# Three of the 44 weight units of the gated product in other matmul forms: 512 columns, 384 columns, and two row tiles per block

## The chip, the cores and the metric

The kernel runs on one core of one Trainium2 chip. The metric is the device time of one execution in microseconds (us). The engines are TensorE (PE in the rows, with its weight loads as PEld), VectorE (DVE), ScalarE (ACT), GpSimd (POOL) and SyncE (SP), which issues most DMAs.

## The reference, cut to what matters

One layer of a hybrid decoder runs over 520 columns of activations (512 prompt tokens and 8 sample tokens) of width 1024. Three branches are merged and normed into h. Then comes a gated feed-forward part, and the change lies in its first product:

```python
u, new_ffn = causal_dwconv(h @ prm['w_ffn_in'], ffn_buf, prm['ffn_dw'], prm['ffn_dw_b'])   # 1024 -> 2*2816
f = (jax.nn.silu(u[..., :D_FF]) * u[..., D_FF:]) @ prm['w_ffn_out']                        # 2816 -> 1024
out = layer_norm(ALPHA * h + f, prm['ln2_g'], prm['ln2_b'])
```

## The kernel before

**Units.** Activations lie transposed, features on the 128 partitions and the 520 columns free. `w_ffn_in` is cut into 44 weight units (i = 0 to 43) of 128 output features; even ones belong to the gate, odd ones to the other factor. A unit holds eight 128x128 blocks. Weights and activations are each split into a rounded part and a remainder (`hi`, `lo`, type fp32r), and each block is multiplied three times: hi by hi, hi by lo, lo by hi. The 520 columns are worked as two halves of HB = 260. So a unit is two halves of 24 matmuls with 260 columns, first all of half 0, then all of half 1 (`mm3`), each half adding up in a PSUM bank of its own.

**Banks.** All these products take their banks from the pool `pd`, three in all (`PD = 3`), handed out in turn (`dps`). A bank given out anew waits until the readers of its tile before have ended, so the n-th tile waits for the (n-3)-th. Each unit takes two, so unit 8's halves take the banks of unit 6's half 1 and unit 7's half 0, and so on.

**Around a unit.** `wunit` loads the unit by a DMA on SP (`raw`), ScalarE rounds it to `whi`, VectorE makes `wlo`; two buffers each, so the weights of unit i+2 are split when unit i's last matmul is done. `ffn_evac` empties the banks with four instructions of ScalarE: two copies into `u` (tile `fu`) and two scaled and biased ones into `y` (`fy`), halves 0 and 1 each. `ffn_taps` is the convolution along the columns on VectorE. Then come silu, the product of both factors, and the split into `f`, the input of the second product. Units 0 to 5 are handled ahead, half 0 of all, then half 1 of all (`early`).

**Order.** Within TensorE the dense matmuls are chained in the order of the program (`issue_after(last_mm)`). The order of the instructions on ScalarE and VectorE is laid out when the kernel is built, by a planner that simulates the engines and goes by priorities; `hp()` raises one (weight splits, evacuations), dense matmuls have the lowest (`-LOW`). An engine then works in that fixed order.

Of the kernel before, what the change touches and what calls it, by code (L numbers as in the profile page):

```python
# [9 lines left out]
F32 = mybir.dt.float32  # L10
F32R = mybir.dt.float32r
AF = mybir.ActivationFunctionType
ALU = mybir.AluOpType
# [3 lines left out]
HB = 260  # L17
# [99 lines left out]
def build(tc, nc, I, O):  # L117
    V, S, T, G = nc.vector, nc.scalar, nc.tensor, nc.gpsimd
# [4 lines left out]
    LOW = 100000  # L123
# [6 lines left out]
    def hp(more=0):  # L130
        return tc.high_priority(HP + more)
# [6 lines left out]
    pd = st.enter_context(tc.tile_pool(name="pd", bufs=PD, space=bass.MemoryType.PSUM))  # L138
# [6 lines left out]
    def z2(name, shape=(128, NT), dt=F32):  # L145
        return pool.tile(list(shape), dt, tag="z", bufs=NZ, name=name)
# [13 lines left out]
    def act(out, in_, func=AF.Copy, **kw):  # L160
        return S.activation(out, in_, func, **kw)  # L161

    def tt(out, a, b, op):
        return V.tensor_tensor(out, a, b, op=op)  # L164
# [19 lines left out]
    HS = (slice(0, HB), slice(HB, NT))  # L184
# [53 lines left out]
    def wload(src, n):  # L238
        raw = wp.tile([128, 8, 128], F32, tag="raw", bufs=2, name="raw")
        with tc.issue_after(x_load.ins):  # L240
            ins = nc.sync.dma_start(raw[:, :n].rearrange("p k m -> p (k m)"), src)
        nload[0] += 1
        if nload[0] > 1 and late:
            with tc.issue_after(ins.ins):
                late.popleft()()
        elif nload[0] > 6:
            with tc.issue_after(ins.ins):
                cache_step(2 if nload[0] % 3 == 0 else 1)
        return raw

    def wsplit(raw, n, where=None):

        if where is None:
            where = [[wp.tile([128, 8, 128], F32R, tag=t, name=t) for t in ("whi", "wlo")]]
        ks, k0 = [], 0
        for hi, lo in where:
            m = min(hi.shape[1], n - k0)
            if m > 0:
                split(hi[:, :m], lo[:, :m], raw[:, k0:k0 + m])
                ks += [(hi[:, k], lo[:, k]) for k in range(m)]  # L260
            k0 += m
        return ks

    def wunit(src, n, where=None):
        with hp():
            return wsplit(wload(src, n), n, where)
# [8 lines left out]
    with hp():  # L275
# [3 lines left out]
        for k in range(8):  # L279
            xr = t2(f"xr{k}")  # L280
            x_load = nc.sync.dma_start(xr, I['xT'][:, k, :])
            if k < 2:
                q = slice(4 * k, 4 * k + 4)
# [5 lines left out]
    def P(name, i=0, n=1):  # L289
        o = PPO[name] + i  # L290
        return pp[:, o:o + n]
# [52 lines left out]
    last_mm, last_one, nmm, stages = [None], [None], [0], deque()  # L344

    def mm3(ps, w, X, first, last, halves):
        for i, h in enumerate(halves):
            for k, ((hi, lo), (xh, xl)) in enumerate(zip(w, X)):
                for q, (a, x) in enumerate(((hi, xh), (hi, xl), (lo, xh))):
                    with ExitStack() as es:  # L350
                        if last_mm[0] is not None:
                            es.enter_context(tc.issue_after(last_mm[0].ins))
                        nmm[0] += 1
                        if stages and nmm[0] >= NS:
                            es.enter_context(tc.issue_after(stages.popleft().ins))
                            nmm[0] = 0
                        last_mm[0] = T.matmul(ps[i], lhsT=a, rhs=x[:, HS[h]], start=first and k == 0 and q == 0,  # L357
                                              stop=last and k == len(w) - 1 and q == 2)

    def dps(n=2):  # L360
        return [pd.tile([128, 512], F32, tag="d", name="ps")[:, :HB] for h in range(n)]


    def densemm(ps, w, X, first=True, last=True, halves=(0, 1)):
        with tc.high_priority(-LOW):
            mm3(ps, w, X, first, last, halves)

    def dense(w, X):
        ps = dps()
        densemm(ps, w, X)  # L370
        return ps

    zi = [0]

    def zchunk():
        i = zi[0]
        zi[0] += 1
        w = w0 if i == 0 else wunit(I['wz'][i], 8)
        return dense(w, XS)
# [737 lines left out]
    def stream_dense():  # L1117
# [61 lines left out]
        def branch(i, js, na):  # L1179
            br = B_ORDER[i]  # L1180
            wn, X, n, ev = outs[br]
            ahead = []
            for j in js[:na]:
                ahead.append(gate(br, j))
                yield 6.5
            yield ('w', ev)
            for j in js:
                gt = ahead[j] if j < len(ahead) else gate(br, j)
                w = wunit(I[wn][j], n)
                pb = dense(w, X)  # L1190
                if i == 0:
                    mg.append(gt)
                if i == 2:
                    XM.append((t2(f"m{j}h", dt=F32R), t2(f"m{j}l", dt=F32R)))
                with hp():
                    for h in range(2):
                        stt(gt[:, HS[h]], gt[:, HS[h]], 1.0, pb[h], ALU.add, ALU.mult)

                for sl in HS if i == 2 and j == 7 else (slice(0, NT),):
                    if i:  # L1200
                        tt(mg[j][:, sl], mg[j][:, sl], gt[:, sl], ALU.add)
                    if i == 2:
                        hi, lo = [x[:, sl] for x in XM[j]]
                        act(hi, mg[j][:, sl], scale=0.5)
                        last_m[0] = stt(lo, mg[j][:, sl], 0.5, hi.bitcast(F32), ALU.mult, ALU.subtract)
                yield 6.5 + 0.8 * n
# [184 lines left out]
    XH = [(h_hi[:, j, :], h_lo[:, j, :]) for j in range(8)]  # L1391
# [29 lines left out]
    def ffn_taps(c, u, y):  # L1421
        G.tensor_copy(nu[:, c, :], u[:, 510:520])  # L1422
        tt(y[:, 512:520], y[:, 512:520], sfs[:, c, :], ALU.add)
        stt(y[:, 1:512], u[:, 0:511], P('fdw', c * 3 + 1), y[:, 1:512])
        stt(y[:, 2:512], u[:, 0:510], P('fdw', c * 3 + 0), y[:, 2:512])

    def ffn_evac(c, u, y, ps, halves):
        with hp():
            for h, p_ in zip(halves, ps):
                act(u[:, HS[h]], p_)  # L1430
            for h, p_ in zip(halves, ps):
                act(y[:, HS[h]], p_, AF.Identity, scale=P('fdw', c * 3 + 2), bias=P('fdb', c))
# [4 lines left out]
    for h in range(2):  # L1437
        for i in range(NH):
            w, u, y = early[i]
            ps = dps(1)  # L1440
# [6 lines left out]
    def ffn_chunk(c, i):  # L1447
        if i < NH:
            _, u, y = early[i]
        else:  # L1450
            u, y = z2("fu"), z2("fy")
            ffn_evac(c, u, y, dense(wunit(I['wfi'][i], 8), XH), (0, 1))
        ffn_taps(c, u, y)
        return y

    for i in range(22):
        yg = ffn_chunk(i, 2 * i)
        act(yg, yg, AF.Silu)
        yu = ffn_chunk(22 + i, 2 * i + 1)
        tt(yg, yg, yu, ALU.mult)  # L1460
        hi, lo = [t(f"f{i}", dt=F32R) for t in FT[i]]
        split(hi, lo, yg)
        XF.append((hi, lo))
# [123 lines left out]
```

## Time and profile before

| | us |
|---|---|
| median of 3 runs | 1034.26 (1032.29 to 1035.23) |
| profiled execution, its own time | 1034.04 |
| its span in the trace | 1032.3 |
| TensorE busy | 1007.8 (98%) |
| VectorE busy | 710.0 (69%) |
| ScalarE busy | 515.5 (50%) |
| mean granted TensorE clock | 0.993 |

Matmul records overlap each other: one record is some 280 ns long, while the next begins about 120 ns after it. So a busy share near one says that the engine is never empty, and the distance between starts says how fast it goes.

### The profile page before, as it was taken

How to read it: one execution, taken by the hardware profiler on the slowest of the kernel's cores; microseconds unless marked ns; L12 is line 12 of the kernel's file. 1: busy time of each engine (PE TensorE's matmuls, PEld its weight loads, DVE VectorE, ACT ScalarE, POOL GpSimd, SP SyncE). 2: the span in 40 equal slices, each digit the busy share in tenths (PEclk: the TensorE clock that was granted, in tenths of full speed). 3: DMA queues.
4: the chain of work that ended last, by engine and by line, in shares of the span. 5: the costliest groups of instructions: out<-in, count | busy, mean ns of one | idle time of the engine just before them, and what ended most of it. 6: DMA issues, size and time to landing. Idle time of an engine off the chain costs nothing.

```text
span 1032.3 us, 22347 instructions
## 1 busy us (share of the span) xinstructions
PE 1007.8 (98%) x9091; PEld 981.7 (95%) x9091; DVE 710.0 (69%) x1330; ACT 515.5 (50%) x1071; POOL 222.1 (22%) x314
## 2 busy tenths in 40 slices
PE   7999999999999998999999999999999999999995
PEld 7999999999999898889989999999999999999994
DVE  5999899986586699745557688655666556423376
ACT  6255843574543534434544567555555555322264
POOL 0131455464315433311000100111111111000000
PEclk9999999999999999999989999999999999999998
DMA  7543356656438666554424743134343434343222
GB/s 238 188 154 117 133 168 201 210 198 231 161 99 216 212 225 225 160 158 140 134 88 149 267 147 107 57 108 138 108 138 109 138 108 136 113 130 92 84 66 83
DMA packets 48247, 153.10 MB, mean 148 GB/s; under 512 B 9808, under 2 KB 13456, under 8 KB 45072
## 3 DMA queue, kind: packets, MB, share of 16 engines
q1 hardware_dynamic: 34944, 112.18, 33.3%
q0 software_dynamic: 13200, 39.49, 11.7%
q8 instruction: 71, 1.16, 0.5%
q14 instruction: 32, 0.26, 0.1%
HBM read 132.02 MB, written 46.81 MB: 173 GB/s over the span
## 4 chain that ended last, share of the span: by engine, by line
PE 87%; DVE 8%; DMA 2%; issue 1%; ACT 1%; POOL 0%; SPq 0%; ACTq 0%; POOLq 0%; DVEq 0%
PE ps L357 76%; DVE wlo L164 1%; PE at L640 1%; DVE os L1106 1%; PE lor L423 1%; DMA raw<-in_wo_dram 1%; DVE swk L164 1%; DVE r L167 1%; PE pt L496 1%; PE lv L1255 1%; PE po L504 1%; DVE vx L164 1%; DVE acc L167 1%; DMA kx<-in_kx_dram 0%; PE st L821 0%
## 5 line engine op out<-in xcount | busy, mean ns | idle before, releaser
L357 PE MATMUL ps<-x_hi,whi 128*128 128x260 f32 x1024 | 292.5, 286 | 5.4 <-ACT whi L161 5.1
L357 PE MATMUL ps<-x_lo,whi 128*128 128x260 f32 x1024 | 293.0, 286 | 0.3 <-DVE x_lo L164 0.2
L357 PE MATMUL ps<-x_hi,wlo 128*128 128x260 f32 x1024 | 292.2, 285 | 1.0 <-DVE wlo L164 1.0
L164 DVE TENSOR_TENSOR wlo<-raw,whi 128x1024 fp32r<-128x1024 f32 (+2 forms) x152 | 168.1, 1106 | 178.7 <-ACT whi L161 178.3
L161 ACT ACTIVATE whi<-raw 128x1024 fp32r<-128x1024 f32 (+2 forms) x152 | 147.0, 967 | 211.0 <-PE ps L357 184.2
L357 PEld LDWEIGHTS ps<-x_hi,whi 128*128 128x128 f32 x1024 | 194.1, 190 | 6.9 <-ACT whi L161 5.1
L357 PEld LDWEIGHTS ps<-x_hi,wlo 128*128 128x128 f32 x1024 | 194.3, 190 | 2.7 <-DVE wlo L164 1.6
L357 PEld LDWEIGHTS ps<-x_lo,whi 128*128 128x128 f32 x1024 | 193.7, 189 | 1.8 <-DVE x_lo L164 0.9
L357 PE MATMUL ps<-h_lo,whi 128*128 128x260 f32 x640 | 181.3, 283 | 0.0
L357 PE MATMUL ps<-h_hi,whi 128*128 128x260 f32 x640 | 180.8, 283 | 0.0
L357 PE MATMUL ps<-h_hi,wlo 128*128 128x260 f32 x640 | 180.6, 282 | 0.0
L357 PEld LDWEIGHTS ps<-h_hi,wlo 128*128 128x128 f32 x640 | 120.8, 189 | 0.1
L357 PEld LDWEIGHTS ps<-h_lo,whi 128*128 128x128 f32 x640 | 120.5, 188 | 0.1
L357 PEld LDWEIGHTS ps<-h_hi,whi 128*128 128x128 f32 x640 | 120.3, 188 | 0.0
L357 PE MATMUL ps<-f,whi 128*128 128x260 f32 x592 | 108.4, 282 | 0.0
L1422 POOL COPY nu<-fu 128x10 f32<-128x10 f32 x44 | 40.3, 917 | 268.8 <-ACT fu L161 268.8
L357 PEld LDWEIGHTS ps<-f,whi 128*128 128x128 f32 x592 | 91.7, 188 | 0.1
L167 DVE SCALAR_TENSOR_TENSOR acc<-u,pp,acc 128x511 f32<-128x511 f32 (+29 forms) x120 | 84.2, 729 | 0.4
L357 PE MATMUL ps<-f,wlo 128*128 128x260 f32 x296 | 83.5, 282 | 0.0
L167 DVE SCALAR_TENSOR_TENSOR fy<-fu,pp,fy 128x511 f32<-128x511 f32 x88 | 65.7, 747 | 1.5
L161 ACT ACTIVATE fu<-ps 128x260 f32<-128x260 f32 x88 | 33.1, 379 | 45.9 <-PE ps L357 45.7
L357 PEld LDWEIGHTS ps<-f,wlo 128*128 128x128 f32 x296 | 55.7, 188 | 0.0
(574 smaller groups left out, 1920.5 us busy)
## 6 DMA issues: line engine op xcount, KB each, us to landing
raw<-in_wz_dram SPq DMA_DIRECT2D x63, 512.0 KB, 3.8
raw<-in_wfi_dram SPq DMA_DIRECT2D x44, 512.0 KB, 3.5
out_dram<-in_cc_dram SPq DMA_DIRECT2D x128, 128.0 KB, 3.5
rl<-d POOLq DMA_DIRECT2D x32, 256.0 KB, 4.5
raw<-in_wfo_dram SPq DMA_DIRECT2D x16, 512.0 KB, 3.6
out_dram<-in_cb_dram SPq DMA_DIRECT2D x56, 146.0 KB, 3.7
d<-at POOLq DMA_DIRECT2D x16, 256.0 KB, 5.1
raw<-in_wo_dram SPq DMA_DIRECT2D x8, 512.0 KB, 3.8
```

Source lines behind the costliest of these rows:

```text
L161: return S.activation(out, in_, func, **kw)
L164: return V.tensor_tensor(out, a, b, op=op)
L167: return V.scalar_tensor_tensor(out, a, s, b, op0=op0, op1=op1)
L357: last_mm[0] = T.matmul(ps[i], lhsT=a, rhs=x[:, HS[h]], start=first and k == 0 and q == 0, stop=last and k == len(w) - 1 and q == 2)
L423: T.matmul(ps, lhsT=lor[l][w][:, p, :], rhs=X[x][:, HS[h]], start=i == 0, stop=i == len(wx) - 1)
L496: T.transpose(pt[:, a, kb, :], s[a][:, pr, kb * 128:(kb + 1) * 128], ident)
L504: last_po[0] = queue((lambda pr=pr, a=a, kb=kb: T.matmul(po[a * 64:a * 64 + 64, pr * 128:pr * 128 + 128], lhsT=VT(kb, 2 * pr + a), rhs=PTs ...
L640: T.matmul(pst[par][:, c * 128:(c + 1) * 128], lhsT=bk[o:o + 64, c].rearrange("p a b -> p (a b)"), rhs=kr[o:o + 64, c].rearrange("p a b -> ...
L1106: V.tensor_reduce(os2, vx.rearrange("p a b -> p b a"), axis=AX.X, op=ALU.add)
L1255: ins = T.matmul(ps[:, :HB], lhsT=R('ones'), rhs=v, start=first and i == 0, stop=last and i == 1)
L1422: G.tensor_copy(nu[:, c, :], u[:, 510:520])
```

## The change

A new function `dense_form` computes three of the units in other ways; all others stay.

- **Unit 8 (form 512).** Both halves in one go: for each block and each of its three products a matmul of 260 columns into one bank, then one of 512 columns (columns 8 to 519) into another, of which only the last 260 are read.
- **Unit 10 (form 384).** The same with 384 columns (136 to 519).
- **Unit 9 (form "rows").** In half 0 each 128-row matmul becomes two of 64 rows (partitions 0 to 63 and 64 to 127), which add up in two banks; half 1 follows as before. The unit takes three banks. ScalarE copies the second of the two into `u`, VectorE adds the first, and the evacuation of half 0 then reads `u` (a copy onto itself, and `y`).

```diff
+    def dense_form(form, w, X, sm):
+        if form == "rows":
+            ps = out = dps()
+            cut = HS
+            two = pd.tile([128, 512], F32, tag="d", name="ps")[:, :HB]
+            pieces_ = [(0, slice(0, 64)), (0, slice(64, 128))]
+        else:
+            bank = [pd.tile([128, 512], F32, tag="d", name="ps") for h in range(2)]
+            ps = [bank[0][:, :HB], bank[1][:, form - HB:form]]
+            out, cut = [ps[0], bank[1][:, :form]], [slice(0, HB), slice(2 * HB - form, 2 * HB)]
+            pieces_ = [(h, slice(0, 128)) for h in range(2)]
+        last = len(w) - 1
+        with tc.high_priority(-LOW):
+            for k, ((hi, lo), (xh, xl)) in enumerate(zip(w, X)):
+                for q, (a, x) in enumerate(((hi, xh), (hi, xl), (lo, xh))):
+                    for h, r in pieces_:
+                        with tc.issue_after(last_mm[0].ins):
+                            nmm[0] += 1
+                            last_mm[0] = T.matmul(two if r.start else out[h], lhsT=a[r], rhs=x[r, cut[h]],
+                                                  start=k == 0 and q == 0, stop=k == last and q == 2)
+        if form == "rows":
+            densemm(ps[1:], w, X, halves=(1,))
+            act(sm[:, :HB], two)
+            tt(sm[:, :HB], sm[:, :HB], ps[0], ALU.add)
+            ps = [sm[:, :HB], ps[1]]
         return ps
...
-            ffn_evac(c, u, y, dense(wunit(I['wfi'][i], 8), XH), (0, 1))
+            form = {8: 512, 9: "rows", 10: 384}.get(i)
+            w = wunit(I['wfi'][i], 8)
+            ffn_evac(c, u, y, dense(w, XH) if form is None else dense_form(form, w, XH, u), (0, 1))
```

## Rows read from the trace of the kernel before

**Rows 1.** The page's span and busy time: engine, busy us, share, instructions.

```profile
span 1032.3 us, 22347 instructions
PE 1007.8 (98%) x9091; PEld 981.7 (95%) x9091; DVE 710.0 (69%) x1330; ACT 515.5 (50%) x1071; POOL 222.1 (22%) x314
```

**Rows 2.** All waits of TensorE: who waited for whom, us, times, longest.

```profile
PE ps L357 <- ACT whi L161: 5.1, 1, 5.1
PE po L504 <- DVE sav L816: 1.5, 1, 1.5
...
PE ld L1261 <- DVE r L164: 0.5, 1, 0.5
```

**Rows 3.** Busy time by stretch (us, engines, clock, DMA share, GB/s): gated product, units 8 to 10.

```profile
640.00:885.00 245.00, 245.00 (x2047) 245.00 (x2046) 146.30 (x223) 141.57 (x265) 39.47 (x44) 1.00 0.34 112
676.30:693.50 17.20, 17.20 (x146) 17.20 (x145) 10.67 (x16) 8.88 (x16) 2.65 (x3) 1.00 0.36 123
```

**Rows 4.** TensorE in order of time (start, us, form): first matmuls of units 8, 9, 10.

```profile
676.30 0.28 PE L357 MATMUL ps<-h_hi,whi 128*128 128x260 f32 x1
676.42 0.28 PE L357 MATMUL ps<-h_lo,whi 128*128 128x260 f32 x1
...
682.05 0.28 PE L357 MATMUL ps<-h_hi,whi 128*128 128x260 f32 x1
...
687.80 0.28 PE L357 MATMUL ps<-h_hi,whi 128*128 128x260 f32 x1
```

**Rows 5.** The same view where the granted clock is 0.50: spacing of like matmuls.

```profile
538.31 0.42 PE L357 MATMUL ps<-orh,wlo 128*128 128x260 f32 x1
538.52 0.42 PE L357 MATMUL ps<-orh,whi 128*128 128x260 f32 x1
538.74 0.42 PE L357 MATMUL ps<-orl,whi 128*128 128x260 f32 x1
```

**Rows 6.** Matmuls of 64 rows in order of time; one line's durations (min/median/max ns).

```profile
336.88 1.13 PE L464 MATMUL s<-qkv,qkv 64*128 64x256 f32 x8
337.94 0.25 PE L737 MATMUL xu<-X,yt 32*32 32x32 f32 x4
...
L467 PE MATMUL s<-qkv,qkv x64: 272/272/373, 216.5 to 292.5; 64*128 64x128 f32 x64
```

**Rows 7.** ScalarE in order of time [idle before, releaser], from 676 to 690.

```profile
676.38 1.06 ACT L161 ACTIVATE whi<-raw 128x1024 fp32r<-128x1024 f32 x1 [1.16 <-PE ps L357]
677.35 0.37 ACT L161 ACTIVATE fu<-ps 128x260 f32<-128x260 f32 x1
677.62 0.56 ACT L161 ACTIVATE fy<-ps,pp 128x260 f32<-128x260 f32 x1
...
682.13 1.06 ACT L161 ACTIVATE whi<-raw 128x1024 fp32r<-128x1024 f32 x1 [0.51 <-PE ps L357]
683.10 0.65 ACT L161 ACTIVATE fu<-ps 128x260 f32<-128x260 f32 x2
683.63 1.03 ACT L161 ACTIVATE fy<-ps,pp 128x260 f32<-128x260 f32 x2
685.15 0.39 ACT L161 ACTIVATE fu<-ps 128x260 f32<-128x260 f32 x1 [0.48 <-PE ps L357]
685.43 0.56 ACT L161 ACTIVATE fy<-ps,pp 128x260 f32<-128x260 f32 x1
...
687.89 1.06 ACT L161 ACTIVATE whi<-raw 128x1024 fp32r<-128x1024 f32 x1 [0.77 <-PE ps L357]
688.86 0.37 ACT L161 ACTIVATE fu<-ps 128x260 f32<-128x260 f32 x1
689.12 0.56 ACT L161 ACTIVATE fy<-ps,pp 128x260 f32<-128x260 f32 x1
```

**Rows 8.** TensorE in order of time around its gaps, then busy and clock by stretch.

```profile
406.02 1.09 PE L504 MATMUL po<-PT,va 128*64 128x128 f32 x16 [1.52 <-DVE sav L816]
...
534.70 0.39 PE L357 MATMUL ps<-orl,whi 128*128 128x260 f32 x1 [0.82 <-DVE orl L164]
534.93 0.28 PE L357 MATMUL ps<-orh,wlo 128*128 128x260 f32 x1
535.90 0.58 PE L357 MATMUL ps<-orh,whi 128*128 128x260 f32 x1 [0.69 <-ACT orh L161]
...
406.00:408.00 2.00, 1.98 (x45) 1.92 (x45) 2.00 (x6) 0.68 (x3) 0.20 (x2) 1.00 0.37 131
...
536.00:538.00 2.00, 1.83 (x5) 1.05 (x5) 1.38 (x4) 0.42 (x1) 0.00 (x0) 0.50 0.07 25
...
542.00:544.00 2.00, 2.00 (x15) 2.00 (x15) 1.66 (x4) 0.64 (x1) 0.00 (x0) 0.82 0.13 35
```

**Rows 9.** Busy time in the last stretch, after TensorE's last product.

```profile
1020.00:1032.30 12.30, 0.17 (x1) 0.00 (x0) 8.54 (x18) 4.53 (x10) 0.00 (x0) 0.66 0.25 87
```

More of the change, by code (lines that the diff above doesn't have):

```diff
@@ L370, in dense @@
         densemm(ps, w, X)
+        return ps
+    def dense_form(form, w, X, sm):
[23 more added lines that the diff above has]
+            ps = [sm[:, :HB], ps[1]]
         return ps
```

## The prediction

> **What bounds the kernel now.** I read the page's busy times first: TensorE is busy for 1007.8 of 1032.3 us [rows 1]. Then its waits: apart from the start (5.1 us) the longest is 1.5 us, all of the longer ones lie before the gated product, and behind it only 0.5 us is left [rows 2]. Then the stretch of the gated product: 2047 matmuls in 245.00 us without a gap, at a granted clock of 1.00, so 119.7 ns from one to the next; VectorE is busy for 60% and ScalarE for 58% of it [rows 3]. The starts of units 8, 9 and 10 are 5.75 us apart, which is 48 times 119.7 ns [rows 4]. So in this stage TensorE's own pace is the bound, and as nothing behind it waits for anything but TensorE and its results, a microsecond added to TensorE here is one at the end. The profiled execution took 1034.04 us with a span of 1032.3; the sum is made against 1034.04, which is 0.2 us under the median of 1034.26.
>
> **Unit 8, wider half.** 24 matmuls grow from 260 to 512 columns. At a clock of 0.50 (1.2 GHz) the same matmul has a spacing of 216 ns [rows 5], which is 260 columns at one per clock (216.7). At 1.00 (2.4 GHz) one column per clock would be 108.3 ns, so 11.4 ns of the 119.7 are something else. No matmul of this type with 512 columns is in the trace. Lower bound: the 512 columns alone, 213.3 ns, +93.6 ns each, +2.25 us. Upper bound: the spacing grows with the columns (119.7 x 512/260 = 235.7), +116 ns, +2.78 us. I take the 11.4 ns as a fixed addition: 224.7 ns, +105 ns, **+2.52 us**, between the two.
>
> **Unit 10, 384 columns.** In the same way 160.0 to 176.8 ns, +0.97 to +1.37 us, and at 171.4 ns **+1.24 us**.
>
> **No load is saved.** The halves now take turns on one block. But loads and matmuls are equal in number, 9091 each [rows 1], although hi by hi and hi by lo use the same block one after the other; that repeat starts after 0.12 us like any other [rows 4]. A repeated block gives nothing back.
>
> **Unit 9, two row tiles.** 24 matmuls become 48 of 64 rows. The nearest rows are eight of 64 rows by 256 columns, of the other type, in two banks by turns [rows 6]: 128 columns alone last 272 ns, and eight times 256 columns last 1.13 us with the next engine step 1.06 us after their start. One with 256 columns lasts about 376 ns (1.13 us less seven spacings of 108 ns), so 128 columns more cost 104 ns and 256 cost 208. One behind another the eight would need 8 x 208 = 1.66 us; in pairs side by side 4 x 208 = 0.83. They took 1.06, so pairs run together, and 0.23 us went into changing to 64 rows and back. I take **+0.23 us**. Upper bound, if this type doesn't pair: 24 x 119.7 = +2.87 us. Lower: each pair sheds the 11.4 ns, -0.27 us.
>
> **The banks: new waits.** This is where I see most of the cost. A tile waits for the third before it. Before, half 1 of a unit began 2.87 us after half 0, and that hid the emptying. Now count on: unit 8 has tiles 4 and 5, unit 9 tiles 6, 7 and 8, unit 10 tiles 9 and 10.
> - Unit 8's second matmul wants the bank of unit 7's half 0. On the odd unit 9, which has the same place in the loop as unit 7, that half is emptied at 685.99, well before the unit's end at 687.80 [rows 4, 7]. No wait.
> - Unit 9's second matmul writes tile 8, the bank of unit 8's wide half, which ended with the matmul just before. ScalarE's order after an even unit is: split of the weights of the unit after next (682.13), both copies, both scaled copies, ended at 683.63 + 1.03 = 684.66; the unit ended at 682.05 [rows 4, 7]. So the bank is free 2.6 us after the unit's end, and TensorE stands: **+2.6 us**. Behind that matmul all others of the unit queue, half 1 too.
> - Unit 10's second matmul wants tile 7, unit 9's half 1. There the order is split, copy, scaled copy, ended at 689.12 + 0.56 = 689.68 against a unit's end of 687.80 [rows 4, 7]. Unit 10 no longer has 24 matmuls to do first: **+1.8 us** (1.88 less the one matmul that goes ahead).
> - Unit 11's half 1 wants unit 10's half 0, free about 2.1 us after the end, and comes 2.87 us after it. No wait, with 0.8 us to spare.
>
> Both waits shrink by the 1.06 us of the split if the planner lets the emptying go first; that is their lower bound for now (1.5 and 0.7). If the copy, the in-place copy and the scaled copy of unit 9's half 0 come between, the second grows by up to 0.38 + 0.38 + 0.56 = 1.3 us.
>
> **The rest of unit 9.** One copy of ScalarE (0.38 us like `fu` [rows 7]), one sum on VectorE (an estimate of 0.4 us, as the same width costs ScalarE that), and the copy onto itself, which was a copy before. They lie beside half 1 (2.87 us) on engines that are 40% idle: no cost. Without that cover unit 10's first matmul would wait for them, some 0.8 us, but beside the 1.8 us already counted. Weights: units 10 and 11 are split behind units 8 and 9 as before, in 2.2 us with `wlo`, while each unit lasts over 6: no cost. DMAs and POOL are not touched.
>
> **Sum.** 2.52 + 1.24 + 0.23 + 2.6 + 1.8 = 8.4 us; 1034.04 + 8.4 = **1042.4 us**. The unknown sizes alone take it from 2.25 + 0.97 - 0.27 + 1.5 + 0.7 = 5.2 (1039.2) to 2.78 + 1.37 + 0.23 + 2.6 + 3.1 = 10.1 (1044.1).
>
> **Rivals.**
> - *B. The row tiles don't pair.* For: the paired rows are of another type [rows 6]. Against: the 64-row layout and the two banks are alike. It adds 2.87 - 0.23 = 2.6: 1045.0.
> - *C. The emptying goes first, or is hidden.* The planner simulates, sees both banks end at once, and lets it go ahead of the split. For: the order now isn't that of the program (the split of a later unit goes ahead), so simulated times decide it, and these change. Against: after both kinds of unit the split is first [rows 7]. With 2 x 1.06 less it is 1040.3, with no wait at all 1038.0.
> - *D. The clock falls.* At 533 to 536 three gaps close together (0.82 and 0.69 the longest) were followed by a clock of 0.50 until about 542.7; one gap of 1.52 us was not [rows 8]. A stand of 2.6 us and soon another of 1.8 lie between. A like stretch of 6.7 us from 535.9 loses 6.7 x (1 - 119.7/216) = 3.0 us: 1045.4.
> - *E. Columns are not what sets the pace.* If loads set the 119.7 ns and a wide matmul fits in the same spacing, 3.76 us fall away: 1038.7. Against it stands the spacing at 1.2 GHz, one column per clock [rows 5], which puts 512 columns at 213 ns or more.
> - *F. Not slower.* One mechanism: the planner lays out the orders behind unit 8 anew and in doing so shortens the stretch of 12.3 us after TensorE's last product, where VectorE is busy for 8.5 us [rows 9]. From 5.3 us on it would bring the time within 0.3% of now: 1034 to 1037. Against: that chain hangs on the last product only, and nothing in it is touched.
>
> Beside E stands the Trainium skill, "TensorE: Matmul & The Clock Gate", section "Back-to-back issue gap": in a stream of loads and matmuls it gives about 131 ns for one of 512 columns. By it unit 8 would cost 24 x 11 ns = 0.3 us instead of 2.5, and the time would be near E's, but no run here shows it and the rows at 1.2 GHz speak against it.
>
> **How the numbers follow.** Chances: my sum (A) 0.44, B 0.19, C 0.16, D 0.11, E 0.05, F 0.05. The likeliest gives 1042.4. The range goes down to C's end of 1038.0 and up to 1046.2, B or D with the columns at their upper bound and a little of the second wait's growth; outside lie F, and B with D together (1048). About 0.3% (3.1 us) is what a measurement of this kernel can tell from no change. A to E are all above it; F is split into 0.04 within and 0.01 faster.
>
> **What would show it.** In the changed profile the first 48 matmuls of unit 8 should come in pairs of about 344 ns, unit 10's of about 291 ns, unit 9's row tiles 120 ns per pair. TensorE should show a gap of about 2.6 us at unit 9's start and one of about 1.8 us at unit 10's, both put down to ScalarE's `fy`, and none in units 8 and 11. Pairs at 240 ns in unit 9 would be B, a split that comes after the emptying C, a clock of 0.50 behind the gaps D, pairs of 240 ns in unit 8 E. A time under 1038 would make the waits wrong, one over 1046 the pairing and the clock.

## The result, and the profile after

| | before | after |
|---|---|---|
| median of 3 runs, us | 1034.26 | 1039.68 (1039.14 to 1042.84) |
| medians of a later comparison (30 and 7 runs), us | 1034.14 | 1039.54 |
| span of the profiled execution, us | 1032.3 | 1041.1 |
| TensorE busy, us | 1007.8 | 1014.5 |
| start of unit 8 to start of unit 11, us | 17.26 | 23.29 |

The changed kernel takes 1.0066 times as long, with an interval of 1.0048 to 1.0083; in the later comparison 1.0051 (1.0033 to 1.0070). That is 5.4 us more by either pair of medians, where the sum gave 8.4; the 1039.68 lies inside the range, 2.7 us under the value given.

The page of the changed kernel, as in [rows 1]:

```profile
span 1041.1 us, 22400 instructions
PE 1014.5 (97%) x9115; PEld 986.7 (95%) x9115; DVE 710.8 (68%) x1331; ACT 515.7 (50%) x1072; POOL 221.3 (21%) x314
```

Of its waits of TensorE, as in [rows 2], the one in the changed stage, where there was none before:

```profile
PE ps L392 <- ACT fy L161: 1.2, 1, 1.2
```

There are 24 matmuls more, 24 weight loads more, and one new wait on `fy`, where the prediction had two. In order of time TensorE shows where each unit begins (start, us, form; x2 is a pair; L392 is the new function, L357 the old):

```profile
680.00 0.51 PE L392 MATMUL ps<-h_hi,whi 128*128 128x260 f32 x2
...
688.11 0.51 PE L392 MATMUL ps<-h_hi,wlo 128*128 128x260 f32 x2
688.54 0.38 PE L392 MATMUL ps<-h_hi,whi 64*128 64x260 f32 x1
690.15 0.39 PE L392 MATMUL ps<-h_hi,whi 64*128 64x260 f32 x1 [1.22 <-ACT fy L161]
...
692.91 0.40 PE L392 MATMUL ps<-h_hi,wlo 64*128 64x260 f32 x2
693.23 0.39 PE L357 MATMUL ps<-h_hi,whi 128*128 128x260 f32 x1
...
696.19 0.46 PE L392 MATMUL ps<-h_hi,whi 128*128 128x260 f32 x2
...
703.29 0.28 PE L357 MATMUL ps<-h_hi,whi 128*128 128x260 f32 x1
```

Against 5.75 us a unit before [rows 4]: unit 8 lasts 8.47 us (+2.72; its end is taken 0.36 us after the start of its last pair), unit 9 7.72 (+1.97) and unit 10 7.10 (+1.35). That is +6.0 us. Unit 9's part is a gap of 1.49 us (688.54 to 690.15, less 0.12) and 0.48 us besides. Unit 10 starts without a gap. ScalarE in the same stretch, as in [rows 7]:

```profile
688.30 1.06 ACT L161 ACTIVATE whi<-raw 128x1024 fp32r<-128x1024 f32 x1 [2.98 <-PE ps L392]
...
689.54 0.56 ACT L161 ACTIVATE fy<-ps,pp 128x260 f32<-128x260 f32 x1
689.99 0.39 ACT L161 ACTIVATE fu<-ps 128x260 f32<-128x260 f32 x1
...
693.34 0.39 ACT L161 ACTIVATE fu<-ps 128x260 f32<-128x260 f32 x1
...
697.51 0.56 ACT L161 ACTIVATE fy<-ps,pp 128x260 f32<-128x260 f32 x1
```

The first `fy` behind unit 8 ends at 690.10, and TensorE goes on at 690.15. Unit 9's half 1 is emptied only at 698.07, with unit 10 long under way. The two banks of its row tiles are free earlier: ScalarE's copy of the second one is the line at 693.34, and VectorE's sum, which reads the first, ends at 694.19:

```profile
693.76 0.43 DVE L164 TENSOR_TENSOR fu<-fu,ps 128x260 f32<-128x260 f32 x1 [1.21 <-ACT fu L161]
```

The span of this execution grew by 8.8 us, more than these 6.0. It is 3.7 us late before unit 8 begins, where the code is the same: most of it lies at 340 to 360 us, where the granted clock is lower than before (last columns: clock, DMA share, GB/s; the first two rows are of after, the last two of before).

```profile
340.00:350.00 10.00, 10.00 (x137) 8.56 (x135) 5.76 (x12) 5.78 (x19) 5.75 (x9) 0.86 0.94 311
350.00:360.00 10.00, 10.00 (x85) 8.83 (x85) 4.01 (x7) 3.21 (x10) 0.55 (x1) 0.80 0.32 99
```

```profile
340.00:350.00 10.00, 10.00 (x156) 8.77 (x156) 6.18 (x12) 6.71 (x23) 6.19 (x10) 1.00 0.95 305
350.00:360.00 10.00, 10.00 (x131) 8.84 (x130) 6.44 (x18) 4.58 (x15) 1.50 (x3) 1.00 0.40 118
```

From 347 to 354 us the granted clock is 0.51. Two more of the profiles below show such a stretch there and are as late ahead of unit 8 (the changed kernel again, and six units with the second tile from an idle pool), and one shows half of it (rows only). The other ten, with the kernel before and all three forms with an own bank among them, show nothing of it, though the code ahead of unit 8 is the same in all, and the medians differ by 5.4. I count it as chance of the execution; why the clock falls there in some was not studied.

Behind the stage 0.9 us come back. From the first matmul of the second product to the end the changed kernel takes 147.9 us (893.14 to 1041.06), before 148.8 (883.42 to 1032.26). The tail from the start of the last matmul of that product is 14.0 us in both; the difference lies ahead of it, where the last blocks of the second product and the matmuls of the second norm alternate. The order that the planner laid out is not what differs: by the names and shapes in the trace every engine does the same instructions there in the same order, before and after. What differs is a load. ScalarE splits the last piece of `w_ffn_out` when it has landed, and waits for it for 2.26 us before and 0.25 after (first row before, second after):

```profile
993.85 0.85 ACT L161 ACTIVATE wxh<-raw 128x768 fp32r<-128x768 f32 x1 [2.26 <-DMA raw<-in_wfo_dram]
1001.83 0.85 ACT L161 ACTIVATE wxh<-raw 128x768 fp32r<-128x768 f32 x1 [0.25 <-DMA raw<-in_wfo_dram]
```

The time from issue to landing of that load is in the last column, 4.9 us before and 3.0 after:

```profile
raw<-in_wfo_dram SPq DMA_DIRECT2D x1, 384.0 KB, 4.9
raw<-in_wfo_dram SPq DMA_DIRECT2D x1, 384.0 KB, 3.0
```

Behind the late load ScalarE's work for the norm comes up to 1.7 us later, and the norm's matmuls that need it then follow each other more slowly (before, six of them last 1.31 us from 1002.33 on; after, eight last 1.12 from 1011.55), which costs TensorE the 0.9 us. The other profiles agree. In ten of the fourteen this load takes 3.0 to 3.3 us, and the stretch to the end 147.9. In the ladder, with turns in three units, before and with 384 only it takes 4.2, 4.5, 4.9 and 5.0 us, and the stretch 148.2, 148.5, 148.8 and 148.9. Why the load is late stays open: in all four a packet of 16 KB of another queue (kind `instruction`) moves while the load runs, in the changed kernel none, but two of the ten quick loads have such a packet beside them too. Most kernels have one trace, so whether a late load belongs to the kernel or to the execution is not shown, and 0.9 us is less than the medians can tell. The profile's account is 6.0 - 0.9 = 5.1 us, against 5.4 in the medians.

### The profile page after: what moved, and what is told of

Its sections match the earlier page's. It is cut to its first block, busy times and chain, and to the rows that moved or that the text cites. A ratio compares the mean times of both kernels' runs of the same rounds, so it can differ in the third digit from the quotient of the medians.

```text
span 1041.1 us, 22400 instructions
## 1 busy us (share of the span) xinstructions
PE 1014.5 (97%) x9115; PEld 986.7 (95%) x9115; DVE 710.8 (68%) x1331; ACT 515.7 (50%) x1072; POOL 221.3 (21%) x314
## 4 chain that ended last, share of the span: by engine, by line
PE 49%; DVE 2%; DMA 1%; ACT 0%; issue 0%; SPq 0%; ACTq 0%
PE ps L357 45%; PE ps L392 2%; DMA raw<-in_wo_dram 1%; DVE r L167 1%; PE lv L1283 1%; PE ld L1289 0%; DMA out_dram<-S 0%; PE lv L1289 0%; DMA sff<-in_sffn_dram 0%; PE lm L1283 0%; DVE wlo L164 0%; PE ld L1283 0%; DVE ot L167 0%; DVE lrs L1367 0%; DVE orl L164 0%
## 5 line engine op out<-in xcount | busy, mean ns | idle before, releaser
L357 PE MATMUL ps<-x_hi,whi 128*128 128x260 f32 x1024 | 292.8, 286 | 5.5 <-ACT whi L161 4.9
L357 PE MATMUL ps<-x_lo,whi 128*128 128x260 f32 x1024 | 293.1, 286 | 0.3
L357 PE MATMUL ps<-x_hi,wlo 128*128 128x260 f32 x1024 | 292.3, 285 | 1.0 <-DVE wlo L164 1.0
L357 PEld LDWEIGHTS ps<-x_hi,whi 128*128 128x128 f32 x1024 | 194.2, 190 | 7.0 <-ACT whi L161 4.9
L357 PEld LDWEIGHTS ps<-x_hi,wlo 128*128 128x128 f32 x1024 | 194.3, 190 | 2.7 <-DVE wlo L164 1.6
L357 PEld LDWEIGHTS ps<-x_lo,whi 128*128 128x128 f32 x1024 | 193.8, 189 | 1.8 <-DVE x_lo L164 0.9
L357 PE MATMUL ps<-h_lo,whi 128*128 128x260 f32 x600 | 170.0, 283 | 0.0
L357 PE MATMUL ps<-h_hi,whi 128*128 128x260 f32 x600 | 169.6, 283 | 0.0
L357 PE MATMUL ps<-h_hi,wlo 128*128 128x260 f32 x600 | 169.3, 282 | 0.0
L357 PEld LDWEIGHTS ps<-h_hi,wlo 128*128 128x128 f32 x600 | 113.2, 189 | 0.1
L357 PEld LDWEIGHTS ps<-h_lo,whi 128*128 128x128 f32 x600 | 112.9, 188 | 0.1
L357 PEld LDWEIGHTS ps<-h_hi,whi 128*128 128x128 f32 x600 | 112.8, 188 | 0.2
L357 PE MATMUL ps<-f,whi 128*128 128x260 f32 x592 | 108.4, 282 | 0.0
L357 PEld LDWEIGHTS ps<-f,whi 128*128 128x128 f32 x592 | 91.7, 188 | 0.1
L357 PE MATMUL ps<-f,wlo 128*128 128x260 f32 x296 | 83.5, 282 | 0.0
L357 PEld LDWEIGHTS ps<-f,wlo 128*128 128x128 f32 x296 | 55.7, 188 | 0.0
```

## The experiments

The edits are to the line that names the forms (`form = {...}.get(i)`) where nothing else is said. "Gap" is the distance between two starts less one spacing of 0.12 us.

**The parts, one by one.** First the changed kernel again:

> The changed kernel itself, beside its parts on one chip. If the stretch of units 8 to 10 carries the whole change, it is 6.0 us slower than the kernel before (units 8 to 10 lasted 23.29 us in the changed profile, 17.25 before). If the 3.7 us by which its profile was late ahead of unit 8 belong to the change too, it is 8 to 9 us slower and that lateness shows again.

1.0051 (1.0033 to 1.0070). Units 8 to 10 take 23.28 us in its profile. Its profile is again late ahead of unit 8 (by 4.3 us), its median is not.

```diff
-            form = {8: 512, 9: "rows", 10: 384}.get(i)
+            form = {8: 512}.get(i)         # first run
+            form = {9: "rows"}.get(i)      # second
+            form = {10: 384}.get(i)        # third
```

> Only unit 8 in the 512 form. Theory that the spacing grows with the columns (0.455 ns each): pairs of 353 ns, unit 8 lasts 8.46 us, +2.7 us in all if no bank is late. Rival, columns at one per clock and a fixed 11.4 ns: pairs of 344 ns, +2.5 us. Bank theory: unit 9's half 1 takes the bank that unit 8 empties first, free 2.0 us after unit 8, 2.87 us are there: no gap. If the last emptied (2.5 us) and more comes between, a gap of some tenths.

> Only unit 9 in row tiles, unit 8 with its halves one after the other as before. Pairs of 120 ns. Theory that banks are handed out in the order of first use to the one emptied first: the second tile of unit 9 takes unit 8's half 0, whose y ends 2.1 us after unit 8, a gap of about 2.0 us, plus 0.4 to 0.5 us for the change to 64 rows and back: +2.5 us. Rival, in the order of allotment: it waits for half 1's y at 2.6 us: +3.0 us. Rival, the gap came from the interleaving of unit 8: no gap, +0.5 us.

> Only unit 10 in the 384 form. Spacing by columns: pairs of 296 ns, unit 10 lasts 7.10 us, +1.35 us. Rival with a fixed 11.4 ns: 291 ns, +1.24 us. Unit 9 is in the old form, its half 0 is emptied while its half 1 runs, so no gap ahead of unit 10 by either theory of the banks.

| | median, us (before 1034.14) | ratio | unit in the profile, us |
|---|---|---|---|
| 512 only | 1036.94 | 1.0026 (1.0014 to 1.0037) | 8.46, no gap |
| rows only | 1036.20 | 1.0026 (1.0008 to 1.0043) | gap of 2.0, then a low clock |
| 384 only | 1035.63 | 1.0010 (0.9998 to 1.0022) | 7.10, no gap |

The three additions, 2.8, 2.1 and 1.5 us, make 6.4 against 5.4 for all, alike within the intervals; that the parts add up exactly is not shown, as 384 only can't be told from no change. Both wide forms behave as the spacing by columns says. In the run with rows only, TensorE's rows, and then two stretches with their clock (third column from the end), are:

```profile
683.22 0.38 PE L392 MATMUL ps<-h_hi,whi 64*128 64x260 f32 x1
685.34 0.39 PE L392 MATMUL ps<-h_hi,whi 64*128 64x260 f32 x1 [1.73 <-ACT fy L161]
...
686.25 0.63 PE L392 MATMUL ps<-h_hi,whi 64*128 64x260 f32 x2
```

```profile
686.00:688.00 2.00, 2.00 (x24) 2.00 (x22) 1.42 (x3) 0.45 (x1) 0.00 (x0) 0.50 0.72 213
688.00:690.00 2.00, 2.00 (x24) 1.86 (x22) 0.00 (x0) 0.19 (x1) 0.00 (x0) 0.70 0.32 123
```

and ScalarE's in the same run:

```profile
684.18 0.65 ACT L161 ACTIVATE fu<-ps 128x260 f32<-128x260 f32 x2
684.71 1.03 ACT L161 ACTIVATE fy<-ps,pp 128x260 f32<-128x260 f32 x2
```

The second tile goes on at 685.34. The two `fy` begin at 684.71; one takes 0.56 us, so the first ends at about 685.27 and the second at 685.74. It was the first: the tile has the bank that was emptied first, and not the one that the order of allotment gives. And here the clock fell to 0.50 behind the gap, so pairs took 216 ns for a while. Both stretches show it; the unit lasts about 1.6 us more than gap and change of tiles explain. This execution took 1038.23 us, 2.0 more than the median of its twelve, so how many of them had the fall isn't shown.

**The gap taken away.** The second tile comes from another pool, idle in this stage; first with all three forms, then with rows only, then with rows in six units:

```diff
-            two = pd.tile([128, 512], F32, tag="d", name="ps")[:, :HB]
+            two = fg("two")[:, :HB]
```

> All three forms, but the second tile of unit 9 comes from another pool that is idle in this stage, so that unit 9 takes two banks of the pool. If the gap at unit 9 is the wait for a bank, it is gone: unit 9 about 6.2 us instead of 7.7, the three units 21.8 us instead of 23.3, +4.5 us against the kernel before instead of +6.0. If the gap came from changing to 64 rows, it stays.

> Only unit 9 in row tiles, its second tile from the other pool. No gap, clock 1.00 throughout, unit 9 about 6.2 us: +0.4 to 0.5 us, all of it for the change to 64 rows and back. If row tiles themselves bring the clock down (0.50 behind the gap of the run with rows only), it falls here too and the unit lasts some 1.6 us more.

> The same six units with the second tile from the idle pool. No gap and a clock of 1.00 in all of them; 6 x 0.38 = +2.3 us for changing to 64 rows and back. If row tiles bring the clock down without a gap, some of the six last 1.6 us more.

All three forms: 1.0043 (1.0028 to 1.0059); units 8 to 10 take 21.69 us, 1.6 less, and `fy` is gone from TensorE's waits. Rows only: 1.0002 (0.9989 to 1.0015), so the row tiles alone can't be told from no change; six units of them 1.0017 (1.0005 to 1.0030), 1036.44 against 1034.18, with no wait on `fy`. That is the 2.3 us expected, but since 0.9 us comes back behind the stage in its profile, the agreement is worth no more than its interval. The 0.38 us of a unit rest on the trace; the run with one such unit shows where they go (`two` is the second tile):

```profile
681.59 0.28 PE L357 MATMUL ps<-h_hi,wlo 128*128 128x260 f32 x1
681.79 0.38 PE L392 MATMUL ps<-h_hi,whi 64*128 64x260 f32 x1
681.80 0.38 PE L392 MATMUL two<-h_hi,whi 64*128 64x260 f32 x1
...
682.02 0.28 PE L392 MATMUL two<-h_lo,whi 64*128 64x260 f32 x1
...
684.66 0.28 PE L392 MATMUL ps<-h_hi,wlo 64*128 64x260 f32 x1
684.87 0.39 PE L357 MATMUL ps<-h_hi,whi 128*128 128x260 f32 x1
685.09 0.28 PE L357 MATMUL ps<-h_lo,whi 128*128 128x260 f32 x1
```

Two tiles start together, and pairs follow every 120 ns. Four spacings are longer, two at each change of tile size: 0.20, 0.23, 0.21 and 0.22 instead of 0.12.

**The ladder of columns.** Units 8, 12, 16, 20 and 24 in the wide form:

```diff
+            form = {8: 260, 12: 320, 16: 384, 20: 448, 24: 512}.get(i)
```

> Five even units with wider second matmuls: units 8, 12, 16, 20, 24 with 260, 320, 384, 448, 512 columns. Spacing by columns (0.455 ns each): pairs of 239, 266, 295, 324, 353 ns. A fixed 11.4 ns and 0.417 ns per column: 239, 264, 291, 318, 344. Columns alone, one per clock: 239, 253, 280, 306, 333. Turns with 260 columns cost nothing by themselves in all three.

First and last pair of the units with 260, 384 and 512 columns, and where the next unit starts:

```profile
676.38 0.41 PE L392 MATMUL ps<-h_hi,whi 128*128 128x260 f32 x2
681.90 0.41 PE L392 MATMUL ps<-h_hi,wlo 128*128 128x260 f32 x2
682.15 0.28 PE L357 MATMUL ps<-h_hi,whi 128*128 128x260 f32 x1
...
723.04 0.46 PE L392 MATMUL ps<-h_hi,whi 128*128 128x260 f32 x2
729.84 0.46 PE L392 MATMUL ps<-h_hi,wlo 128*128 128x260 f32 x2
730.13 0.28 PE L357 MATMUL ps<-h_hi,whi 128*128 128x260 f32 x1
...
772.42 0.51 PE L392 MATMUL ps<-h_hi,whi 128*128 128x260 f32 x2
780.53 0.51 PE L392 MATMUL ps<-h_hi,wlo 128*128 128x260 f32 x2
780.88 0.28 PE L357 MATMUL ps<-h_hi,whi 128*128 128x260 f32 x1
```

23 distances each give pairs of 240.0, 266.5, 295.7, 323.9 and 352.6 ns. Less 120.0 for the narrow one, the wide ones take (to some 0.3 ns) 120.0, 146.5, 175.7, 203.9 and 232.6: a straight line with 0.447 ns per column (112.6 over 252) and 4 ns left over. The fixed 11.4 ns fall, and so does one column per clock (0.417).

**Row tiles in turn.** All 24 matmuls of rows 0 to 63, then the 24 of rows 64 to 127 (the loop over `pieces_` put outside for this form):

```diff
-                    for h, r in pieces_:
+            for part in ([[p] for p in pieces_] if form == "rows" else [pieces_]):
...
+                        for h, r in part:
```

> As the changed kernel, but in unit 9 the 24 matmuls of rows 0 to 63 come first and the 24 of rows 64 to 127 after them. If tiles of different rows overlap only when they are neighbours in the order, each takes 120 ns: 5.7 us for the 48 instead of 2.9. The second bank is wanted 2.87 us later, so the gap is gone. Rival: 64 rows are faster in themselves, about 60 ns each in any order.

One run of 1039.83 us. The 64-row matmuls now follow one by one, but for a few where the first rows end and the second begin, which overlap:

```profile
684.86 0.28 PE L393 MATMUL ps<-h_lo,whi 64*128 64x260 f32 x1
684.98 0.28 PE L393 MATMUL ps<-h_hi,wlo 64*128 64x260 f32 x1
...
690.02 0.28 PE L393 MATMUL ps<-h_hi,wlo 64*128 64x260 f32 x1
690.23 0.39 PE L357 MATMUL ps<-h_hi,whi 128*128 128x260 f32 x1
```

The 48 take 5.6 us instead of 2.9. A tile of 64 rows is no faster; only its neighbour with the other rows runs beside it.

**Turns without columns or row tiles.**

```diff
+            form = {8: 260, 9: 260, 10: 260}.get(i)          # first run
+            form = 260 if 8 <= i < 20 else None              # second
```

> Units 8, 9 and 10 all with halves taking turns and 260 columns each: no added column, no row tiles. Theory of first use: unit 8 no gap; the second matmul of unit 9 wants the bank that unit 8 empties first, free about 2.0 us after its end, a gap of 1.5 to 2.0 us; the same for unit 10 behind unit 9; none in unit 11. Sum +3 to 4 us, all of it waiting. Rival, the order of allotment: for two tiles a unit it names the same banks, so the same gaps. Rival, that the waits hang on the added columns: no gap and +0.0.

> Units 8 to 19 with halves taking turns and 260 columns, no row tiles. Each unit but the first waits for the bank that the unit before empties first: eleven gaps of 1.5 to 2.0 us, +18 to +22 us in all. If a gap of 2 us is enough by itself to bring the clock to 0.50, it falls behind several of the eleven, and such a unit lasts 1.6 to 3 us more. If the fall behind the two row-tile runs needed the row tiles after the gap, the clock stays at 1.00 through all of them.

Three units: 1.0051 (1.0037 to 1.0066), as much as the whole change. Unit 8 has no gap, units 9 and 10 have 1.96 and 1.68 us; the three last 21.15 us instead of 17.26. Twelve units: 1054.23 against 1035.87, one run each; eleven waits on `fy`, 17.0 us together. The first two of them, and a stretch behind the first:

```profile
683.65 0.39 PE L392 MATMUL ps<-h_hi,whi 128*128 128x260 f32 x1 [1.80 <-ACT fy L161]
...
692.71 0.39 PE L392 MATMUL ps<-h_hi,whi 128*128 128x260 f32 x1 [1.52 <-ACT fy L161]
```

```profile
686.00:688.00 2.00, 2.00 (x11) 2.00 (x11) 0.00 (x0) 0.51 (x1) 0.00 (x0) 0.50 0.46 180
```

Behind the first gap (1.96 us) the clock fell, with matmuls of 128 rows. Behind the other ten (1.68 us each) it stayed at 1.00. With three units the clock stayed at 1.00 behind a first gap of the same 1.96 us, though both kernels have the same code up to there.

**Rows in six units.**

```diff
+            form = {9: "rows", 15: "rows", 21: "rows", 27: "rows", 33: "rows", 39: "rows"}.get(i)
```

> Row tiles in units 9, 15, 21, 27, 33 and 39, all else as before. Each has a gap of about 2.0 us as in the run with rows only, and 0.4 us for the change to 64 rows: +14.4 us if the clock stays at 1.00. If a gap of this size brings the clock to 0.50, each unit that it hits lasts about 1.6 us more, up to +24 us; if one was chance, one in six or none.

1.0041 (1.0028 to 1.0054), +4.4 us, far from the 14.4 expected. Only unit 9 has a gap (2.0 us, and the clock fell behind it); the other five have none. ScalarE around the start of unit 15 at 721.01:

```profile
718.54 0.56 ACT L161 ACTIVATE fy<-ps,pp 128x260 f32<-128x260 f32 x1
...
721.00 1.06 ACT L161 ACTIVATE whi<-raw 128x1024 fp32r<-128x1024 f32 x1 [0.51 <-PE ps L357]
...
722.23 0.56 ACT L161 ACTIVATE fy<-ps,pp 128x260 f32<-128x260 f32 x1
```

Here the planner lets half 0 of the unit before be emptied by 719.10, while its half 1 still runs; for unit 8 it put that behind the unit's end. My expectation had taken unit 8's order for that of every even unit. Unit 15 also settles who gets which bank: by the order of allotment its second tile would have waited for half 1's `fy`, until 722.79. It didn't wait: the pair of both tiles (x2) starts at once.

```profile
721.01 0.39 PE L392 MATMUL ps<-h_hi,whi 64*128 64x260 f32 x2
```

The runs agree with a bank being given out when a tile is first used. Whether the banks then go round in that order, or the one that is emptied first goes first, no run tells apart.

## Why the prediction was right or wrong

The frame held: TensorE's pace bounds the stage, and what units 8 to 10 gained in length is the change (6.0 us in the profile, of which 0.9 come back behind it; 5.4 in the medians). The value of 8.4 us came out too high through the banks: of 4.4 us of waits 1.5 came. That 1039.68 lies in the range is in part luck. The unknown sizes of the sum alone, with both waits, began at 5.2 us, hardly under the 5.4 measured, and the range's low end of 1038.0 was drawn for rival C, whose order didn't come.

- **Columns: mechanism right, size a little low.** 2.52 us were 2.72 and 1.24 were 1.35. The step that failed is the choice between the bounds: the rest of 11.4 ns was taken as fixed, where the ladder shows nearly all of it to grow with the columns. The upper bounds (2.78 and 1.37) were almost the values.
- **No load saved: right.** Taking turns with 260 columns gives unit 8 in the ladder 5.77 us against 5.75.
- **Row tiles pair: right, rival B falls.** Pairs come every 120 ns, and in turn each takes 120. The change of tiles, 0.23 by the nearest rows, measured 0.38 in the run without a gap.
- **The gap at unit 9: right place, wrong size.** 2.6 us were 1.49. Two causes: the second tile has the bank that is emptied first, not unit 8's wide half (in the changed kernel TensorE went on at 690.15; ScalarE's first `fy` is at 689.54 and lasts 0.56), and the planner put this `fy` ahead of the second copy (at 689.99). With rows only, where the order of the copies was the old one, the gap was 2.0. Rival C's order (emptying ahead of the split) did not come: the split at 688.30 is still first.
- **The gap at unit 10: wrong, there is none.** The failing step is "a tile waits for the third before it", counted in the order of allotment. The runs agree with the order of first use: unit 9's two row-tile banks, used before its half 1 and free at 694.19, went to unit 10. That half 1 was emptied only at 697.51 + 0.56 = 698.07, while unit 10 had both its banks at 696.19. That the wait itself is real where a bank is short, the runs with turns show: 1.7 to 2.0 us a unit.
- **Rival D, the clock: not here, but near.** In the two profiles of the changed kernel the gap was 1.5 us and units 8 to 10 show no fall. At 2.0 us it fell in three of four profiled cases, and cost 1.5 to 1.7 us each time. By these cases a gap of 2.6 us, as in my sum, would have deserved a higher chance than 0.11; no run has a gap that long in this stage.
- **Rival E, the pace not set by columns: falls.** 512 columns took 232.6 ns. The figure of the Trainium skill ("TensorE: Matmul & The Clock Gate", section "Back-to-back issue gap"), about 131 ns, does not hold for these matmuls.
- **Rival F: falls in its cause.** 0.9 us did come back behind the stage, where 5.3 would have been needed, but the engines do the same work there in the same order, and the tail behind the last product is 14.0 us as before. What came back was the wait for a late load. The prediction's premise that nothing behind the stage waits for anything but TensorE and its results overlooked it: in the profile before, ScalarE waits 2.26 us for that load.

So two errors of 1.1 and 1.8 us on the banks went one way, and 0.6 us on columns and tiles the other: 8.4 - 2.9 + 0.6 = 6.1 against 6.0 in the trace. With the 0.9 us that came back it would be 5.2, against medians of 5.4.

## What to carry to other kernels

Halves that take turns on one block finish together, so nothing hides the emptying of their banks: with three banks that alone cost 1.7 to 2.0 us a unit, more than 64-row tiles (0.4 us) or 124 columns too many (1.35 us). Before counting such a wait, find out which bank a tile really gets, and read the emptying order at that very unit, not at a neighbour. A tile from an idle pool removed the wait at once.

## What the runs showed of the hardware that was not expected

- In this type the spacing is 0.447 ns per column at a clock of 1.00 (2.4 GHz), not 0.417, and linear from 260 to 512 columns; at 1.2 GHz it was one column per clock [rows 5]. Why is open.
- Behind gaps of 1.96 to 2.0 us the clock fell to 0.50 (1.2 GHz) in three of four profiled cases, which cost 1.5 to 1.7 us each time; behind the eleven gaps of 1.68 us it stayed at 1.00 (2.4 GHz). That the length of the gap decides is not shown: the same 1.96 us behind the same code brought a fall once and none once, and each of the shorter gaps followed another gap. The row tiles are not needed for it: it fell behind matmuls of 128 rows too, and with six units of row tiles without a gap it did not fall in that stage.
- The same load of 384 KB, issued at the same place, took 3.0 us in one kernel and 4.9 in another, and with the same order of instructions on every engine that moved the end by 0.9 us.
